# A hybrid decoder layer: gates of the recurrence in two groups of two chunks, 1/rms of the queries in the softmax's scale, that of the values in their copy, and the tail's last sum kept apart

## The chip, the cores and the metric

The kernel runs on one core of one Trainium2 chip. The metric is the device time of one execution in microseconds; of the kernel before there are three runs, and their median is compared. Besides the runs there is one profiled execution, whose trace gives every instruction of every engine with its start and its duration.

## The reference

The reference is one layer of a decoder trunk on x of 512 tokens by 1024 features, in float32:

```
x = x + 0.5 * rms_norm(swiglu(rms_norm(x, ..), ffn1_w_gu, ffn1_w_down), ..)
y = hybrid_mixer(rms_norm(x, mix_pre_g), w_in, ...)
x = x + rms_norm(y, mix_post_g)
x = x + 0.5 * rms_norm(swiglu(rms_norm(x, ..), ffn2_w_gu, ffn2_w_down), ..)
```

The mixer multiplies its normed input h by w_in and takes five parts out of the product: x_lru and gate_lru (512 columns each), q (8 heads of 64), k and v (2 heads of 64 each).

- The recurrence: a causal convolution of width 4 over x_lru gives xc; two block-diagonal products (8 blocks of 64 by 64) with a sigmoid give r and i; a = exp(8 r log_sigmoid(lambda)); u = sqrt(1 - a^2) * i * xc; then the scan h[t] = a[t] h[t-1] + u[t], times gelu(gate_lru).
- The attention: a sliding window of 128 over blocks of 128 queries, with a sink per head: m = max(max(scores), sink), p = exp(scores - m) / (sum + exp(sink - m)), and p times v.

Both results are normed, put side by side and multiplied by w_o.

rms_norm(x)[token] is x[token] * 1/rms(x[token]) * gain. The factor 1/rms is one number for each token, so q, k, v and x_lru of a token can all be computed from the input without it, and be multiplied by it afterwards. A score is q . k, so the factor of a query can as well stand in the scale of its row of scores; the factor of a value belongs to that value's row.

## The kernel before

Every product of float32 matrices is made of three matmuls of rounded halves: weights and activations are split into a high and a low part (ACT casts the high part, DVE or POOL subtracts it for the low part), and high*high, high*low and low*high are summed in PSUM (`mm3`, lines 505 to 507). The order of the instructions on each engine is written out by hand, in the order of the program; weights come through a list of units (`W.take`, `W.fill`), which loads, casts and splits a few units ahead. The loads go through SP's queue.

The feed-forward parts before and after the mixer are long rows of such products, in a form with seven products for eight. What is changed stands in the mixer and at the very end.

The mixer's first part keeps features on the partitions and tokens on the free axis, in tiles of 128x512:

- `boundary` ends with the four products of x_lru (tiles `an`), then PE computes k (`pk`), v (`pv`) and the four query products (`pq0` to `pq3`, two heads each), 24 matmuls of 512 columns each.
- `mx.R` holds 1/rms of every token, the same row on all partitions; `scaled(t, b)` is DVE's multiply of a product by it (line 1426). It is used for x_lru (line 1434), k, v and the four query tiles. `InvRms.invert` makes the factor first as a column per block of 128 tokens (`rs`, line 558), before it is turned into the row.
- `conv` (ACT line 1442, DVE line 1446) makes xc of two chunks of 128 channels at a time; `split_xc` (lines 1472 and 1473) makes its high part on ACT and its low part on POOL.
- `lru_gates(ci)` does one chunk: six matmuls (line 1454) whose weights lie in 64 of the 128 rows, the two halves of a chunk at the same time in the two halves of the array; two sigmoids on ACT (`r`, `other`); and because the halves of the two gates come out on the wrong partitions, two DMAs on SP's queue that gather `ig` (lines 1457 and 1459), POOL's product u = ig * xc (line 1461) and a DMA on POOL's queue that puts `other` into `r` (line 1462). It is called once for each chunk, after the query product of the same number.
- `in_parts` (lines 1426, 1486, 1492, 1493) scales a query or key product, copies its first block for the first block of the attention (tile `home`), and splits it. The low part of the last query tile is put off (`deferred`) until the attention has begun.
- After the first gates PE turns v (`vt`, line 1512), and DVE copies it into `home` (line 1514).
- The attention goes over 8 units (block b, group n of four heads): `scores` (PE products `cur` at line 1610 for the first block, `sc` at line 1621 for the others; DVE masks them, takes the maximum and makes `nm`, the negative of the maximum times the scale, line 1641), `exps` (ACT, line 1652, one for each head), `turn_p` (PE transposes, line 1664), `values` (lines 1683 and 1684). Between them PE does the products of the recurrence's gate (`gt`).

Small tiles of the tag "w" (`wt`) share 8 buffers in turn, so that a new one waits until the one before in its buffer is read; PSUM has 8 banks in the same manner.

The end of the kernel goes over four blocks of 128 tokens (tb). For each piece of the output DVE adds the last product to what was summed so far (`yp`, line 1983), ACT squares and sums it (line 1984), DVE or POOL multiplies by the gain (`last`, line 1988), and when all pieces are there: the sum of the sums (`tot`, lines 1986, 1990, 1992), the square root on ACT (1995), the reciprocal (1996) and the last multiply and add (1999) on DVE, and the store (2000). The last block has three pieces, of 512, 256 and 256 columns.

## Time and profile before

| what | value |
|---|---|
| median of three runs | 845.98 us (845.3 to 846.42) |
| span of the profiled execution, first to last instruction | 843.6 us |
| granted TensorE clock, mean | 0.998 |
| PE busy | 834.5 us, 99% of the span |
| DVE / ACT / POOL busy | 732.7 / 523.8 / 201.7 us |
| chain that ended last | 97% PE |

The profiled execution has no time of its own beside its span; what lies around the span is taken as the difference between the median of the runs and the span, 2.4 us.

Views of the trace used below: the page (spans, busy time, the chain that ended last), the chain in order of time (start, length, engine, tile, line), the timeline (start, length, engine, line, operation, output <- inputs, shapes, count; in brackets how long the engine was idle before and what ended that) and the list of one tile's instructions. A PE matmul row gives the time that one matmul is in the array, and matmuls overlap; their pace is read from the starts, or from the chain, where each stands with its share.

### The profile page before, as it was taken

The page shows a single profiled execution, that of the slowest core. Times are in us where ns is not written, and L with a number is a line of the kernel's source. Part 1 is how long each engine was busy: PE and PEld are TensorE (multiplying, and loading weights), DVE is VectorE, ACT ScalarE, POOL GpSimd, SP SyncE. Part 2 cuts the span into 40 slices and gives each one's busy share as a digit, 9 for nine tenths or more (in the row PEclk, how much of TensorE's full clock was granted, in tenths as well). Part 3 has the DMA queues.
Part 4 walks back from the last instruction along what each step waited for, and adds up shares of the span by engine and source line. Part 5 has one row for each costly group of instructions (what it writes and reads, how often), then busy time and mean ns, then how long its engine had stood idle before and what let it go on. Part 6 is the DMA issues. An engine that isn't in the chain of part 4 may idle for free.

```text
span 843.6 us, 12618 instructions
## 1 busy us (share of the span) xinstructions
PE 834.5 (99%) x4568; PEld 722.6 (86%) x4568; DVE 732.7 (87%) x1020; ACT 523.8 (62%) x874; POOL 201.7 (24%) x214
## 2 busy tenths in 40 slices
PE   9999999999999999999999999999999999999996
PEld 8988888988988998997788899888888888888885
DVE  4978999998979865889899589799998998998996
ACT  6646856666666655456788457436757767666552
POOL 2023000140320333334646055112004113032001
PEclk9999999999999999999999999999999999999999
DMA  7249419397595799222511131169539939769742
GB/s 251 77 131 348 151 59 322 80 254 254 129 248 185 169 261 343 77 79 91 158 50 51 50 110 42 50 137 273 186 108 231 322 91 249 249 154 262 295 137 101
DMA packets 123615, 143.75 MB, mean 170 GB/s; under 512 B 23896, under 2 KB 81568, under 8 KB 123040
## 3 DMA queue, kind: packets, MB, share of 16 engines
q1 hardware_dynamic: 109232, 111.86, 41.6%
q0 software_dynamic: 14176, 30.94, 17.0%
q8 instruction: 36, 0.59, 0.3%
q14 instruction: 27, 0.22, 0.1%
q10 hardware_dynamic: 144, 0.13, 0.0%
HBM read 100.45 MB, written 40.89 MB: 168 GB/s over the span
## 4 chain that ended last, share of the span: by engine, by line
PE 97%; ACT 1%; DVE 1%; DMA 1%; issue 0%; POOL 0%; DVEq 0%; POOLq 0%; ACTq 0%
PE ab L955 10%; PE aa L955 10%; PE da L955 5%; PE db L955 5%; PE yaa L1345 3%; PE bb L955 3%; PE ba L955 3%; PE yda L1345 2%; PE ya L507 2%; PE ya L505 2%; PE ya L506 2%; PE a_first L1205 1%; PE aa L885 1%; PE yab L1875 1%; PE yab L1874 1%; PE yab L1876 1%
## 5 line engine op out<-in xcount | busy, mean ns | idle before, releaser
L1115 POOL DMA_DIRECT2D yp_a<-stage x42 | 36.9, 1085 | 181.2 <-ACT stage L1112 160.9
L1115 POOL DMA_DIRECT2D yp_b<-stage x42 | 36.4, 1091 | 144.6 <-ACT stage L1112 121.1
L505 PE MATMUL ya<-hha,whi_ad 128*128 128x512 f32 x62 | 24.1, 389 | 0.0
L506 PE MATMUL ya<-hla,whi_ad 128*128 128x512 f32 x62 | 24.1, 389 | 0.0
L507 PE MATMUL ya<-hha,wlo_ad 128*128 128x512 f32 x62 | 24.1, 389 | 0.0
L688 POOL TENSOR_TENSOR acca_r<-acca_r,sq_r 128x512 f32<-128x512 f32 x6 | 8.2, 1359 | 51.4 <-ACT sq_r L536 51.4
L1988 POOL TENSOR_TENSOR last<-yp,grow 128x512 f32<-128x512 f32 x3 | 3.9, 1290 | 57.7 <-DVE yp L1983 57.7
L524 PE MATMUL an<-xh_mx,whi_xl 128*128 128x256 f32 x64 | 15.8, 287 | 0.0
L1984 ACT ACTIVATE ysq<-yp 128x512 f32<-128x512 f32 (+1 forms) x9 | 5.3, 585 | 16.5 <-DVE yp L1983 16.0
L525 PE MATMUL an<-xh_mx,wlo_xl 128*128 128x256 f32 x64 | 15.5, 283 | 0.0
L505 PE MATMUL gt<-xh_mx,whi_gt 128*128 128x512 f32 x32 | 14.2, 444 | 0.0
L1112 ACT COPY stage<-yab 128x512 f32<-128x512 f32 x12 | 6.5, 604 | 11.7 <-DMA yp_b<-stage 7.4
L507 PEld LDWEIGHTS ya<-hha,wlo_ad 128*128 128x128 f32 x62 | 11.6, 188 | 2.4
L506 PEld LDWEIGHTS ya<-hla,whi_ad 128*128 128x128 f32 x62 | 11.6, 188 | 2.4
L505 PEld LDWEIGHTS ya<-hha,whi_ad 128*128 128x128 f32 x62 | 11.6, 188 | 2.4
L536 ACT ACTIVATE sq_r<-yp_a 128x256 f32<-128x256 f32 (+1 forms) x10 | 5.0, 502 | 12.9 <-DVE yp_a L678 5.9
L505 PE MATMUL pq<-xh_mx,whi_q 128*128 128x512 f32 x32 | 12.8, 400 | 0.0
L505 PE MATMUL pub<-xh_f,whi_bu 128*128 128x512 f32 x32 | 12.6, 395 | 0.0
L507 PE MATMUL gt<-xh_mx,wlo_gt 128*128 128x512 f32 x32 | 12.6, 394 | 0.0
L505 PE MATMUL pgb<-xh_f,whi_bg 128*128 128x512 f32 x32 | 12.6, 393 | 0.0
L506 PE MATMUL gt<-xl_mx,whi_gt 128*128 128x512 f32 x32 | 12.5, 392 | 0.0
L580 ACT ACTIVATE xh_f<-xT,cols 128x256 fp32r<-128x256 f32 x16 | 8.1, 509 | 7.0 <-DVE xT L719 6.4
(2014 smaller groups left out, 3535.0 us busy)
## 6 DMA issues: line engine op xcount, KB each, us to landing
yp_a<-stage POOLq DMA_DIRECT2D x50, 256.0 KB, 8.9
yp_b<-stage POOLq DMA_DIRECT2D x50, 256.0 KB, 9.2
h_a<-za SPq DMA_DIRECT2D x16, 256.0 KB
hxa<-h_a SPq DMA_DIRECT2D x16, 256.0 KB
h_b<-zb SPq DMA_DIRECT2D x16, 256.0 KB
hxb<-h_b SPq DMA_DIRECT2D x16, 256.0 KB
xn<-in_x SPq DMA_DIRECT2D x8, 256.0 KB
xT_hbm<-xT POOLq DMA_DIRECT2D x2, 1024.0 KB, 9.7
```

Source lines behind the costliest of these rows:

```text
L505: pe.matmul(ps, hi[:, k, :], xh, start=start, stop=False)
L506: pe.matmul(ps, hi[:, k, :], xl, start=False, stop=False)
L507: pe.matmul(ps, lo[:, k, :], xh, start=False, stop=stop)
L524: pe.matmul(ps[:, sl], hi[:, k, :], xh, start=k == 0, stop=False)
L525: pe.matmul(ps[:, sl], lo[:, k, :], xh, start=False, stop=False)
L885: pe.matmul(o, w[:, k, js], x, start=first and i + j + k == 0, stop=k == 3 and i == 2, skip_group_check=True)
L955: pe.matmul(b[tb], x[:, blk], w[:, k, :], start=first and q + k + j == 0, stop=q + k == 2 and j == 2, skip_group_check=True)
L1115: pool.dma_start(o, st.rearrange("p (a b) -> p a b", a=2) if len(o.shape) == 3 else st, accum_op=ALU.add)
L1205: pe.matmul(banks[j][:, HALF[0]], ws[j][part][:, k, :], n1.xs[k][xpart][:, HALF[0]], start=k == 0 and part == xpart, stop=stop and k == KD ...
L1345: pe.matmul(o, a[:, k, ms], x[:, js], start=first and i + k + m % 2 == 0, stop=k == 1 and i == 2, skip_group_check=True)
L1874: pe.matmul(banks[i], hh[:, js], hi[:, k, :], start=first and k == 0, stop=False, skip_group_check=True)
L1875: pe.matmul(banks[i], hh[:, js], lo[:, k, :], start=False, stop=False, skip_group_check=True)
```

## The change

Four things are changed.

1. `lru_gates` takes a group of chunks. It issues the matmuls of both chunks, term by term, then all sigmoids and SP's DMAs of the group, then what is handed in as `between`, and last POOL's products and POOL's DMAs. It is called twice: chunks 0 and 1 after the first query product (with the splits of chunks 2 and 3 as `between`), chunks 2 and 3 after the third. The split of chunk 1 stands before v's product now.
2. The query products are no longer scaled: `in_parts` reads the PSUM bank directly. Three small tiles hold the column of 1/rms per block (`rows_scale`) and that times 1/8 and -1/8; `nm` and the exponentials take their scale from them.
3. v is copied out of PSUM by ACT (`act.copy`) without the scale, and the copy of the turned v into `home` multiplies by the column.
4. At the very end, the last piece's sum of squares has a tile of its own, the sum of the first two and the epsilon are made by DVE ahead as the bias of the square root, and the gain multiplies of the last two pieces stand behind the square root in the program.

```diff
--- before.py
+++ after.py
@@ -554,7 +554,7 @@
             n = self.name
             rms = small.tile([P, 2], F32, tag="rms", name=f"rms_s{n}")
             act.activation(rms, ms, AF.Sqrt, bias=self.eps, scale=scale)
-            rs = small.tile([P, 2], F32, tag="rs", name=f"rs_{n}")
+            rs = self.rs = small.tile([P, 2], F32, tag="rs", name=f"rs_{n}")
             dve.reciprocal(rs, rms)
             self.dg = wt(f"dg_{n}", T)[:, :2 * P].rearrange("p (a b) -> p a b", a=2)
             dve.tensor_tensor(self.dg, ident.unsqueeze(1).to_broadcast([P, 2, P]), rs.unsqueeze(2).to_broadcast([P, 2, P]), op=ALU.mult)
@@ -1445,25 +1445,32 @@
                 ci = c0 + j
                 dve.scalar_tensor_tensor(xcs[ci], xps[ci][:, 1 + w:1 + w + T], col("conv_w", w * KC + ci), xcs[ci], op0=ALU.mult, op1=ALU.add)
 
-    def lru_gates(ci):
-
-        banks = bank(f"rg{ci}"), bank(f"ig{ci}")
-        (hi, lo), (xh, xl) = gw["both"], xc_parts[ci]
-        for i, (w, x) in enumerate(((hi, xh), (hi, xl), (lo, xh))):
-            for ps, half in zip(banks, SIDE):
-                pe.matmul(ps, w[half, ci, :], x[half, :], start=i == 0, stop=i == 2)
-        r, other, ig = t2k(f"r{ci}"), wt(f"other{ci}"), wt(f"ig{ci}")
-        act.activation(r, banks[0], AF.Sigmoid, bias=col("b_rg", ci))
-        sync.dma_start(ig[SIDE[0], :], r[SIDE[1], :])
-        act.activation(other, banks[1], AF.Sigmoid, bias=col("b_ig", ci))
-        sync.dma_start(ig[SIDE[1], :], other[SIDE[0], :])
-        u = xcs[ci]
-        pool.tensor_mul(u, ig, u)
-        pool.dma_start(r[SIDE[1], :], other[SIDE[1], :])
-        t = t2k(f"th{ci}")
-        rs_.append(r)
-        us_.append(u)
-        th.append(t)
+    def lru_gates(cs, between=lambda: None):
+
+        banks = {ci: (bank(f"rg{ci}"), bank(f"ig{ci}")) for ci in cs}
+        hi, lo = gw["both"]
+        for i in range(3):
+            for ci in cs:
+                xh, xl = xc_parts[ci]
+                w, x = ((hi, xh), (hi, xl), (lo, xh))[i]
+                for ps, half in zip(banks[ci], SIDE):
+                    pe.matmul(ps, w[half, ci, :], x[half, :], start=i == 0, stop=i == 2)
+        gates = {}
+        for ci in cs:
+            r, other, ig = gates[ci] = t2k(f"r{ci}"), wt(f"other{ci}"), wt(f"ig{ci}")
+            act.activation(r, banks[ci][0], AF.Sigmoid, bias=col("b_rg", ci))
+            sync.dma_start(ig[SIDE[0], :], r[SIDE[1], :])
+            act.activation(other, banks[ci][1], AF.Sigmoid, bias=col("b_ig", ci))
+            sync.dma_start(ig[SIDE[1], :], other[SIDE[0], :])
+        between()
+        for ci in cs:
+            r, other, ig = gates[ci]
+            u = xcs[ci]
+            pool.tensor_mul(u, ig, u)
+            pool.dma_start(r[SIDE[1], :], other[SIDE[1], :])
+            rs_.append(r)
+            us_.append(u)
+            th.append(t2k(f"th{ci}"))
 
     xc_parts = {}
 
@@ -1480,9 +1487,18 @@
     xps = [conv_in(ci, b) for ci, b in enumerate(xl_banks)]
     k0, q0 = home[0][:, :P], home[0][:, T:2 * T]
 
+    rows_scale = const.tile([P, NB], F32, name="rows_scale")
+    score_scale = const.tile([P, NB], F32, name="score_scale")
+    minus_scale = const.tile([P, NB], F32, name="minus_scale")
+    for h in range(2):
+        blocks = slice(2 * h, 2 * h + 2)
+        dve.tensor_copy(rows_scale[:, blocks], mx.rms[h].rs)
+    dve.tensor_scalar(score_scale, rows_scale, HD ** -0.5, None, op0=ALU.mult)
+    dve.tensor_scalar(minus_scale, rows_scale, -HD ** -0.5, None, op0=ALU.mult)
+
     def in_parts(b, first, name, low=dve):
 
-        x = scaled(wt(name), b)
+        x = scaled(wt(name), b) if name == "kT" else b
         dve.tensor_copy(first, x[:, :P])
         if name == "qT3":
             spare.extend(fours("attn", F32R))
@@ -1496,22 +1512,25 @@
     conv(0, xps)
     split_xc(0)
     kT = in_parts(pk, k0, "kT", pool)
+    split_xc(1)
     pv = in_product("pv")
-    vT = scaled(wt("vT"), pv)
+    vT = wt("vT")
+    act.copy(vT, pv)
     conv(2, xps)
     qT = []
     for j in range(4):
         b = in_product(f"pq{j}")
-        if j < KC - 1:
-            split_xc(j + 1)
-        lru_gates(j)
+        if j == 0:
+            lru_gates((0, 1), lambda: (split_xc(2), split_xc(3)))
+        if j == 2:
+            lru_gates((2, 3))
         qT.append(in_parts(b, q0[:, j * P:(j + 1) * P], f"qT{j}", deferred if j == 3 else dve))
         if j == 0:
             vt = bank("vt")
             for b in range(NB):
                 pe.transpose(vt[:, b * P:(b + 1) * P], vT[:, b * P:(b + 1) * P], ident)
             v = home[0][:, 3 * T:]
-            dve.tensor_copy(v, vt)
+            dve.tensor_tensor(v4(v), v4(vt), rows_scale.unsqueeze(2).to_broadcast([P, NB, P]), op=ALU.mult)
     preload(AF.Exp)
 
 
@@ -1592,7 +1611,6 @@
         dve.tensor_tensor_scan(hl[ci], rs_[ci], us_[ci], initial=0.0, op0=ALU.mult, op1=ALU.add)
 
 
-    scale = HD ** -0.5
     yns = []
     ssq = const.tile([P, NB], F32, name="ssq")
     unit = {}
@@ -1638,7 +1656,7 @@
                 dve.tensor_reduce(mx_[:, 2 * i:2 * i + 2], cur, op=ALU.max, axis=AX.X)
                 heads += [both[:, j, 1, :] for j in range(2)]
         nm = small.tile([P, 4], F32, tag="nm", name=f"nm{b}{n}")
-        dve.scalar_tensor_tensor(nm, mx_, -scale, nsink[:, 4 * n:4 * n + 4], op0=ALU.mult, op1=ALU.min)
+        dve.scalar_tensor_tensor(nm, mx_, minus_scale[:, b:b + 1], nsink[:, 4 * n:4 * n + 4], op0=ALU.mult, op1=ALU.min)
         es = small.tile([P, 4], F32, tag="es", name=f"es{b}{n}")
         dve.tensor_add(es, nm, sinks[:, 4 * n:4 * n + 4])
         unit[b, n] = heads, nm, es
@@ -1649,7 +1667,7 @@
         sc = wt(f"sc{b}{n}")
         for j in range(4):
             hs = slice(j * P, (j + 1) * P)
-            act.activation(sc[:, hs], heads[j], AF.Exp, bias=nm[:, j:j + 1], scale=scale, accum_out=dsum[:, j:j + 1])
+            act.activation(sc[:, hs], heads[j], AF.Exp, bias=nm[:, j:j + 1], scale=score_scale[:, b:b + 1], accum_out=dsum[:, j:j + 1])
         act.activation(es, es, AF.Exp)
         if n == 0:
             unit[b] = small.tile([P, 8], F32, tag="den", name=f"den{b}")
@@ -1981,18 +1999,24 @@
             out_products(tb, i, range(f0 + 2 * ((tb, i) in started), f1))
             y = parts[tb, dh][:, c0:c1]
             dve.scalar_tensor_tensor(y, place(tb, i), -1.0 if dh else 1.0, y, op0=ALU.mult, op1=ALU.subtract if dh else ALU.add)
-            act.activation(wt(f"ysq{tb}{i}")[:, :c1 - c0], y, AF.Square, accum_out=ss[:, i:i + 1])
-            if end and i == 2:
-                dve.tensor_add(tot, ss[:, 0:1], ss[:, 1:2])
+            if i == 2:
+                ss_last = small.tile([P, 1], F32, tag="tot", name="ss_last")
+                act.activation(wt(f"ysq{tb}{i}")[:, :c1 - c0], y, AF.Square, accum_out=ss_last)
+                dve.tensor_scalar(tot, ss[:, 0:1], 4.0 / D, 4 * EPS, op0=ALU.mult, op1=ALU.add)
+                dve.scalar_tensor_tensor(tot, ss[:, 1:2], 4.0 / D, tot, op0=ALU.mult, op1=ALU.add)
+            else:
+                act.activation(wt(f"ysq{tb}{i}")[:, :c1 - c0], y, AF.Square, accum_out=ss[:, i:i + 1])
             last.append(wt(f"last{tb}{i}")[:, :c1 - c0])
-            (dve if end or i else pool).tensor_mul(last[i], y, grow[dh][:, c0:c1])
+            if not end or i == 0:
+                (dve if end or i else pool).tensor_mul(last[i], y, grow[dh][:, c0:c1])
+        rs = small.tile([P, 1], F32, tag="rs1", name=f"rs_b{tb}")
         if end:
-            dve.tensor_add(tot, tot, ss[:, 2:3])
+            act.activation(rs, ss_last, AF.Sqrt, bias=tot, scale=4.0 / D)
+            for i, (dh, c0, c1) in list(enumerate(pieces[tb]))[1:]:
+                dve.tensor_mul(last[i], parts[tb, dh][:, c0:c1], grow[dh][:, c0:c1])
         else:
             dve.tensor_add(tot, ss[:, 0:1], ss[:, 1:2])
-
-        rs = small.tile([P, 1], F32, tag="rs1", name=f"rs_b{tb}")
-        act.activation(rs, tot, AF.Sqrt, bias=eps4, scale=4.0 / D)
+            act.activation(rs, tot, AF.Sqrt, bias=eps4, scale=4.0 / D)
         dve.reciprocal(rs, rs)
         for i, (dh, c0, c1) in enumerate(pieces[tb]):
             y = parts[tb, dh][:, c0:c1]
```

## The prediction

> **What bounds the kernel now.** I read the page first, then the chain in order of time around the gates, then the timelines of ACT, POOL and DVE there, and last the chain of the tail. From the page:
>
> ```profile
> span 843.6 us, 12618 instructions
> ...
> PE 834.5 (99%) x4568; PEld 722.6 (86%) x4568; DVE 732.7 (87%) x1020; ACT 523.8 (62%) x874; POOL 201.7 (24%) x214
> ...
> PE 97%; ACT 1%; DVE 1%; DMA 1%; issue 0%; POOL 0%; DVEq 0%; POOLq 0%; ACTq 0%
> ```
>
> PE is the chain. Work taken off another engine gains nothing by itself; an edit counts where it changes PE's own row of instructions, makes PE wait or wait less, or stands behind PE's last matmul. What lies around the span is 845.98 - 843.6 = 2.4 us; I take it as unchanged, so every term below goes from the span to the median as it is.
>
> **Part 1: the gates' groups on PE.** The chain in order of time at the gates of chunk 1:
>
> ```profile
> 395.49 0.42 PE rg L1454
> 395.92 0.23 PE ig L1454
> 396.38 0.43 PE pq L505
> 396.81 0.23 PE pq L506
> ```
>
> A matmul of 512 columns takes 0.23 us of the chain (two gate matmuls, one in each half of the array, share it), but the first after a change between 128-row and 64-row weights takes 0.42 or 0.43. Going into the gates and out again costs 0.42 + 0.43 - 2 x 0.23 = 0.39 us. Before, PE goes in and out after pq0, pq1 and pq2; after pq3 the gates run straight into `cur`, which is 64-row too, so there is one way in and one way out of both together. After, it goes in and out behind pq0 and pq2, and pq3 goes straight into `cur`, again once in and out. One pair goes: **-0.39 us**. The 24 gate matmuls stay. Bounds: 0 (if a group of two breaks the sharing or the pair moves elsewhere) and -0.8 (if two pairs went, which the order of the instructions excludes).
>
> **Part 2: v copied by ACT.** PE turns v behind the first gates, now twelve matmuls instead of six, and waits for ACT's copy instead of DVE's multiply.
>
> ```profile
> 385.15 0.62 ACT L1492 CAST kTh<-kT 128x512 fp32r<-128x512 f32 x1 [0.58 <-DVE kT L1426]
> 385.67 2.00 ACT L209 CAST whi_q<-raw_q 128x1024 fp32r<-128x1024 f32 x2
> 387.57 1.04 ACT L209 CAST whi_gt<-raw_gt__4051 128x1024 fp32r<-128x1024 f32 x1
> 388.52 1.52 ACT L1442 ACTIVATE xc<-xp,cols 128x512 f32<-128x512 f32 x2
> ```
> ```profile
> 389.33 0.66 PE L1512 MATMUL vt<-ident,vT 128*128 128x128 f32 x4
> ```
>
> On DVE four tiny operations (the columns' copies and scales) now stand ahead of the convolution; a 128x1 operation takes 0.16 (row 838.24 below), and back to back they take less, so 0.45 in all (bounds 0.3 and 0.64). kTh slips by that to 385.60. From start to start ACT takes 0.52 for a cast of 512 columns and (387.57 - 385.67)/2 = 0.95 for one of 1024: the cast of chunk 1 (new here) starts at 386.12, two of whi_q at 386.64, whi_gt at 388.54, vT at 389.49, and vT is there at 389.49 + 0.62 = 390.1. PE would turn v at 389.33 + 3 x 0.23 = 390.0. **+0.1 us**, bounds 0 and 0.5. Chunk 1's low part on POOL (two operations of 1.3 ahead of it, done about 388.9) is wanted at 389.2: just covered.
>
> **Part 3: what the second group brings late.** This is the new wait that I take most seriously. `r3` and `other3` moved ahead of qT2's cast on ACT, and in the new order `other3` takes the buffer that `other1` had, which is free only when POOL's DMA of chunk 1 has read it. That DMA stands behind POOL's xcl2, xcl3, u0, its DMA, and u1. Behind `other3` on ACT stands qT2's high part; DVE waits for that with qT2's low part, then makes a wlo_gt of 1.2, and only then copies the first block of pq3, which PE's last matmuls of `cur` read. POOL's rows before, and the operations of DVE beside two of them, and the landing of the DMAs of `r` and `ig`:
>
> ```profile
> 396.66 1.31 POOL L1461 TENSOR_TENSOR xc<-ig,xc 128x512 f32<-128x512 f32 x1 [3.76 <-DMA ig<-other]
> 397.90 0.56 POOL L1462 DMA_DIRECT2D r<-other  x1
> 399.37 2.16 POOL L1473 TENSOR_TENSOR xcl<-xc,xch 128x512 fp32r<-128x512 f32 x1 [0.92 <-ACT xch L1472]
> 402.90 1.75 POOL L1461 TENSOR_TENSOR xc<-ig,xc 128x512 f32<-128x512 f32 x1 [1.36 <-DMA ig<-other]
> ...
> 407.07 2.36 POOL L1461 TENSOR_TENSOR xc<-ig,xc 128x512 f32<-128x512 f32 x1 [0.63 <-DMA ig<-other]
> ```
> ```profile
> 399.17 1.21 DVE L214 TENSOR_TENSOR wlo_gt<-raw_gt__4051,whi_gt 128x1024 fp32r<-128x1024 f32 x1
> ...
> 402.28 1.22 DVE L214 TENSOR_TENSOR wlo_gt<-raw_gt__4099,whi_gt 128x1024 fp32r<-128x1024 f32 x1
> ```
> ```profile
> DMA to landing us min/median/max: 2.3/2.9/3.1
> ```
>
> A POOL operation takes 1.3 alone and about 2.2 when a wlo_gt of DVE started just ahead of it. ACT after vT: two conv starts, a cast of 1024, the table load (1.28), four sigmoids at 0.59 from start to start, so chunk 2's high part starts at 396.1 and is there at 396.7. POOL: xcl2 to 398.1, xcl3 to 399.3; wlo_gt, due at 399.0, then holds u0 up from 399.3 to 400.5, u0 to 401.75, its DMA 0.55 to 402.3; the next wlo_gt (from 402.05) holds u1 up to 403.25, u1 to 404.5. POOL's DMA of chunk 1 starts there and lands 2.3 later, at 406.9. `other3` runs to 407.6 (0.68), qT2's high part to 408.1, its low part (from 408.2, 0.6 to the next) and wlo_gt (1.2, and 0.25 behind POOL's u2) to 410.3, the copy of 0.2 to 410.5. PE wants it for the last quarter of `cur`: pq3's last matmul starts at 408.7, `cur` runs about 1 us behind it, so its last quarter is due at 409.85. **+0.6 us**. Bounds: 0, where u0 and u1 take 1.3 each and the copy waits for pq3 alone; and 3.2, where both xcl take 2.16, both u 2.36 and the DMA 3.1 (landing at 409.5 and all behind it 2.6 later). I take the middle way because the two wlo_gt fall beside u0 and u1 by their own times.
>
> The skill weighs in here. The Trainium skill, "SBUF — State Buffer", section "Who interferes with whom", says that a DVE instruction with two SBUF inputs and a GpSimd instruction that reads SBUF exclude each other for the whole instruction, the first to start winning, while one with at most one SBUF input does not contend. By that rule the queries' low parts, which now read one operand from PSUM, leave POOL alone, and the wait stays 0.6; if they held POOL up as a wlo_gt does, two of them at 0.68 would make it about 2.0 and the sum +0.95. No row before shows such a pair overlapping.
>
> **Part 4: the first unit of the attention.** ACT's sigmoids of chunk 3 used to stand ahead of the exponential's table load; the first transposes waited for the exponentials:
>
> ```profile
> 413.85 0.74 PE L1664 MATMUL pt<-ident,sc 128*128 128x128 f32 x4
> ```
> ```profile
> 437.66 0.60 PE L1664 MATMUL pt<-ident,sc 128*128 128x128 f32 x4
> ```
>
> Unhindered the four take 0.60, here 0.74. The two sigmoids (1.2 us) are gone from this place, and the table load starts behind the cast of pq3: **-0.14 us** (bounds -0.14 and 0, the latter if part 3 delays that cast by more than a microsecond).
>
> **Part 5: five scale multiplies leave DVE, ACT gets a copy.** 5 x 0.68 = 3.4 us less on DVE, 0.6 more on ACT. Nothing on the path: PE runs on through all of them. The factor as a tile instead of a constant in `nm` and in the exponentials, and in v's second copy: the same shapes, **0** (bounds -0.1 and +0.3 for 32 exponentials at 0.01).
>
> **Part 6: the tail.** PE's last matmul, and then DVE and ACT:
>
> ```profile
> 836.39 0.28 PE L1852 MATMUL ybl<-whi_br,hlb 128*128 128x256 f32 x1
> ```
> ```profile
> 836.56 0.42 DVE L1988 TENSOR_TENSOR last<-yp,grow 128x256 f32<-128x256 f32 x1
> 836.91 0.42 DVE L1983 SCALAR_TENSOR_TENSOR yp<-ybl,yp 128x256 f32<-128x256 f32 x1
> 837.24 0.15 DVE L1986 TENSOR_TENSOR tot_b<-ss_b 128x1 f32<-128x1 f32 x1
> 837.36 0.43 DVE L1988 TENSOR_TENSOR last<-yp,grow 128x256 f32<-128x256 f32 x1
> 838.24 0.16 DVE L1990 TENSOR_TENSOR tot_b<-tot_b,ss_b 128x1 f32<-128x1 f32 x1 [0.45 <-ACT ysq L1984]
> 838.76 0.16 DVE L1996 RECIPROCAL rs_b<-rs_b 128x1 f32<-128x1 f32 x1 [0.36 <-ACT rs_b L1995]
> ```
> ```profile
> 837.70 0.42 ACT L1984 ACTIVATE ysq<-yp 128x256 f32<-128x256 f32 x1 [0.56 <-DVE tot_b L1986]
> 838.02 0.19 ACT L1984 ACTIVATION_READ_ACCUMULATOR ysq<-yp 128x1 f32 x1
> 838.43 0.29 ACT L1995 ACTIVATE rs_b<-tot_b,eps 128x1 f32<-128x1 f32 x1 [0.23 <-DVE tot_b L1990]
> ```
>
> All of this is on the path. (a) The last add waits behind a gain multiply; without it, it starts when PE is done, 836.7 instead of 836.91. (b) The square starts at 837.70 because it waits for a sum of the same tile; with a tile of its own it follows the add by 0.5, at 837.2. (c) The square root need not wait for DVE's last sum: 837.2 + 0.51 = 837.75 instead of 838.43. (d) The reciprocal follows by 0.33, at 838.1 instead of 838.76. What moves in between on DVE are two sums (0.16 each) and two gain multiplies (0.34 each from start to start), 837.1 to 838.1: they just fit, and may push the reciprocal by 0.05. **-0.62 us**, bounds -0.7 and -0.4.
>
> **The sum.** -0.39 + 0.1 + 0.6 - 0.14 + 0 - 0.62 = -0.45 us: a span of 843.6 - 0.45 = 843.15 and, with 2.4 around it, 845.5 us. All good ends give -0.39 - 0.14 - 0.7 = -1.2 (-1.3 with part 5's), all bad ends +3.6.
>
> **Rivals.**
> - *No wait at `cur`*: POOL gets through undisturbed, part 3 is 0: -1.05, 844.9 us. For it: u0 took 1.31 once. Against it: wlo_gt of 1.2 comes by at those times.
> - *The wait at `cur` takes the gain and more*: the same chain with POOL's long rows. Each microsecond that POOL's DMA of chunk 1 lands later than 406.3 costs PE one. The kernel is slower by over 0.2% (1.7 us) from a wait of 2.75 on, a landing at 409.0; at the full 3.2 it gives +2.15, 848.1 us. For it: 2.16 and 2.36 stand in the trace. Against it: all four operations would have to be long, and DVE has 3.4 us less to do.
> - *A stall of the late attention goes too*. ACT's two table loads make PE wait at the seventh unit:
>
> ```profile
> 442.41 1.38 PE L1664 MATMUL pt<-ident,sc 128*128 128x128 f32 x4 [0.28 <-ACT sc L1652]
> ```
> ```profile
> 434.38 0.37 ACT L1652 ACTIVATE sc<-sc,nm 128x128 f32<-128x128 f32 x1 [1.59 <-PE po L1683]
> ```
>
> The four transposes take 1.38 instead of 0.60 and start 0.45 late, 1.2 in all. If ACT came to them early by what it saves, this would go: -1.05 - 1.2 = -2.25, 843.7 us. Against it: the row of 434.38 shows ACT idle for 1.59 until PE is there, and what follows is ACT's own row; it moves with PE.
>
> **How the numbers follow.** My forecast (a short wait at `cur`) has 0.50, no wait there 0.22, the long wait 0.14, the late stall gone 0.14. The likeliest gives 845.5 (its own range 844.6 to 846.4). Leaving out the ends of the last two, the range is 843.8 to 847.4. 0.2% is 1.7 us, about what a measurement of this kernel can tell from no change: within it lie the first two and a part of the others, 0.74; faster 0.15, slower 0.11.
>
> **What would show it.** Right: one pair of 0.42 and 0.43 fewer in the chain between pq0 and `cur`; the last 1999 starting 0.6 us closer to PE's last matmul; `cur` longer than its 1 us with DVE's copy of pq3 as what PE waits for, and ACT's `other3` idle until POOL's DMA. Wrong: a wait of PE at the second group of gates or at `vt` of more than 0.5, exponentials longer than 0.35 to 0.38, or a stall of PE in the attention that differs from 1.2.

## The result and the profile after

The changed kernel takes 851.68 us (median of 4 executions, 851.31 to 854.97) against 845.68 for the kernel before: slower by a ratio of 1.0077, 95% interval 1.0061 to 1.0093. The forecast was 845.5, with 847.4 as the upper end of its range. The page of the changed kernel, the rows that answer to those shown of before:

```profile
span 853.3 us, 12607 instructions
...
PE 838.7 (98%) x4568; PEld 722.7 (85%) x4568; DVE 730.3 (86%) x1019; ACT 525.5 (62%) x875; POOL 200.9 (24%) x214
...
PE 62%; issue 14%; DMA 12%; DVE 5%; POOL 3%; ACT 3%; SPq 1%; DVEq 0%; POOLq 0%; ACTq 0%
```

PE was 97% of the chain before and is 62% now; DMA is 12% of it, most of that POOL's `yp_b<-stage` from 595 us on, where no line was changed. (In the second profile, e2 below, the chain is 75% PE and 6% DMA.) The profiled execution is the slowest of the four (854.97; the other three have spans of 849.6 to 850.3): PE waits 2 us at 318 us and then runs at half its pitch for about 3 us. The two windows below are the wait and what follows it; behind the length stand the busy times of PE, PEld, DVE, ACT and POOL, then PEclk (the granted clock), the DMA share and GB/s:

```profile
317.00:320.20 3.20, 1.50 (x7) 0.92 (x5) 1.45 (x3) 2.23 (x5) 0.00 (x0) 1.00 1.10 356
320.20:325.00 4.80, 4.63 (x13) 3.53 (x14) 3.52 (x6) 2.54 (x5) 0.00 (x0) 0.68 1.14 271
```

A second profile of the changed kernel (run e2 below, span 849.9) has a shorter wait there and no fall of the clock, so I compare that one with a second profile of the kernel before (run e1, span 843.8). In both kernels PE executes the same 4568 matmuls, so I cut the trace at the same matmuls: the first of `pv` opens the mixer, the first of `wo` closes its attention. In us, by the starts of these matmuls, counted from the start of the span (worked out from the trace):

| stretch | before (e1) | changed (e2) | difference |
|---|---|---|---|
| start to `pv` (no instruction changed) | 377.3 | 379.8 | +2.6 |
| `pv` to `wo` (gates, queries, attention) | 80.7 | 82.8 | +2.1 |
| `wo` to PE's last matmul (no instruction changed) | 378.6 | 380.8 | +2.2 |
| last matmul to the end of the span | 7.2 | 6.5 | -0.7 |

(The last row is from the two pages and the tails shown in the prediction and below, 843.6 - 836.39 and 853.3 - 846.77.) So 4.8 us come from stretches in which nothing was changed, 2.1 from the mixer, where I had expected +0.17 in all, and the tail gave back 0.7.

In the unchanged stretches the DMAs are slower. From the trace's record of every packet: the 8,192 packets of 512 bytes that the hardware queue moves between 100 and 300 us (pieces of weights, which are loaded as 128 columns of 4 bytes) take 32.3 ns on average in e1 and 37.5 in e2, and the 10,752 packets of 2 KB of POOL's queue (sums of products, added into memory) take 178.6 and 187.8. The 512-byte packets of the first 100 us are slower too (27.2 and 30.1), hundreds of microseconds before the first changed instruction.

In the mixer, the groups of the exponentials, before and after (minimum, median and maximum in ns of one):

```profile
L1652 ACT ACTIVATE sc<-sc,nm x24: 356/369/406, 419.7 to 447.0; 128x128 f32<-128x128 f32 x24
L1652 ACT ACTIVATE sc<-cur,nm x8: 350/370/381, 412.7 to 416.5; 128x128 f32<-128x128 f32 x8
```
```profile
L1670 ACT ACTIVATE sc<-sc,nm,score_scale x24: 447/458/487, 425.0 to 453.7; 128x128 f32<-128x128 f32 x24
L1670 ACT ACTIVATE sc<-cur,nm,score_scale x8: 446/458/469, 417.6 to 421.7; 128x128 f32<-128x128 f32 x8
```

Each got 0.09 us longer by taking its scale from a tile. The late stall at the seventh unit, 1.38 for the four transposes before, is now

```profile
448.62 1.65 PE L1682 MATMUL pt<-ident,sc 128*128 128x128 f32 x4 [0.55 <-ACT sc L1670]
```

And the wait at `cur` is there. PE's rows, before and after:

```profile
409.33 1.05 PE L1610 MATMUL cur<-home 64*128 64x128 f32 x16
410.31 0.50 PE L505 MATMUL gt<-xh_mx,whi_gt 128*128 128x512 f32 x1
```
```profile
413.84 0.94 PE L1628 MATMUL cur<-home 64*128 64x128 f32 x12
415.05 0.49 PE L1628 MATMUL cur<-home 64*128 64x128 f32 x4 [0.27 <-DVE home L1502]
415.47 0.50 PE L505 MATMUL gt<-xh_mx,whi_gt 128*128 128x512 f32 x1
```

The chain in order of time at that place (start, duration, what):

```profile
408.65 2.23 DMA r<-other
...
410.99 0.69 ACT other L1463
411.68 0.49 ACT qT2h L1508
...
412.19 0.69 DVE qT2l L1509
412.88 1.92 DVE wlo_gt L214
414.80 0.21 DVE home L1502
...
415.05 0.49 PE cur L1628 x4
```

It is link by link the chain of part 3 of the prediction: POOL's DMA of chunk 1, `other3`, the cast of the third queries, their low part, a `wlo_gt`, the copy, PE. From the first matmul of `cur` to the next product it is 1.63 us here and 1.48 in e2, against 0.98 before. One link is longer than forecast, `wlo_gt`, and these rows show beside what; the earlier pair is POOL's product u of chunk 1 with the `wlo_gt` before it:

```profile
407.21 2.60 DVE L214 TENSOR_TENSOR wlo_gt<-raw_gt__4110,whi_gt 128x1024 fp32r<-128x1024 f32 x1
412.19 0.69 DVE L1509 TENSOR_TENSOR qT2l<-pq,qT2h 128x512 fp32r<-128x512 f32 x1 [2.17 <-ACT qT2h L1508]
412.80 2.00 DVE L214 TENSOR_TENSOR wlo_gt<-raw_gt__4110,whi_gt 128x1024 fp32r<-128x1024 f32 x1
```
```profile
407.42 1.30 POOL L1469 TENSOR_TENSOR xc<-ig,xc 128x512 f32<-128x512 f32 x1
412.42 1.29 POOL L1469 TENSOR_TENSOR xc<-ig,xc 128x512 f32<-128x512 f32 x1 [3.23 <-DMA ig<-other]
```

POOL's products take 1.3, as alone; both `wlo_gt`, 1.21 alone, end 1.09 us behind the product beside them. The low part `qT2l`, which reads one operand from PSUM, runs beside the second product and neither is longer than alone.

The tail, PE's last matmul and the engines behind it:

```profile
846.77 0.28 PE L1870 MATMUL ybl<-whi_br,hlb 128*128 128x256 f32 x1
```
```profile
847.09 0.42 DVE L2001 SCALAR_TENSOR_TENSOR yp<-ybl,yp 128x256 f32<-128x256 f32 x1 [0.18 <-PE ybl L1870]
...
848.42 0.15 DVE L2020 RECIPROCAL rs_b<-rs_b 128x1 f32<-128x1 f32 x1
848.61 1.54 DVE L2023 SCALAR_TENSOR_TENSOR yp<-last,rs_b,x_rows 128x512 f32<-128x512 f32 x3
```
```profile
847.55 0.42 ACT L2004 ACTIVATE ysq<-yp 128x256 f32<-128x256 f32 x1
...
848.09 0.29 ACT L2014 ACTIVATE rs_b<-ss_last,tot_b 128x1 f32<-128x1 f32 x1
```

The last step starts 848.61 - 846.77 = 1.84 us behind PE's last matmul; before it was 838.96 - 836.39 = 2.57.

### The profile page after: what moved, and what is told of

It reads as the page before. It is cut to its first block, busy times and chain, and to the rows that moved or that the text cites. A ratio compares the mean times of both kernels' runs of the same rounds, so it can differ in the third digit from the quotient of the medians.

```text
span 853.3 us, 12607 instructions
## 1 busy us (share of the span) xinstructions
PE 838.7 (98%) x4568; PEld 722.7 (85%) x4568; DVE 730.3 (86%) x1019; ACT 525.5 (62%) x875; POOL 200.9 (24%) x214
## 4 chain that ended last, share of the span: by engine, by line
PE 62%; issue 14%; DMA 12%; DVE 5%; POOL 3%; ACT 3%; SPq 1%; DVEq 0%; POOLq 0%; ACTq 0%
PE aa L955 10%; DMA yp_b<-stage 8%; PE da L955 5%; PE yaa L1345 3%; PE ba L955 3%; PE yda L1345 2%; PE ab L955 2%; DMA raw_ad__3210<-in_ffn_w_down 2%; PE ya L505 2%; PE ya L506 2%; PE ya L507 2%; POOL yp_b L1115 1%; PE wo L1823 1%; DMA raw_second<-in_ffn_w_gu 1%; PE yea L1345 1%
## 5 line engine op out<-in xcount | busy, mean ns | idle before, releaser
L831 ACT CAST hhs<-s4b 128x512 fp32r<-128x512 f32 x4 | 2.5, 621 | 16.3 <-DVE s4b L867 16.3
```

## The experiments

First four kernels together: are the slow packets a matter of the chip and the execution, or of the program; what do the exponentials cost; what does the tail give? Each ratio is to the kernel before, measured beside it on the same chip, with its 95% interval.

**e1, the kernel before once more.** No edit.

> The kernel before, unchanged, once more. In the trace of the changed kernel the DMA packets of 512 bytes take 38.5 ns on average between 100 and 300 us, in that of before 31.7, though the instructions there are the same; and the changed kernel stalls PE by 0.65 us at the first matmul of `ab` in each of four blocks from 603 us on, before does not. Theory A: the pace of the packets belongs to the chip or to the execution and not to the kernel; then this run can show 38 ns too, with the four stalls and 2 to 4 us more than 845.7. Theory B: it belongs to the program as changed (where its data or its code lies); then this run shows 31.7 ns, no stall of that kind, and 845.3 to 846.4.

845.46 us, ratio 1.0001 (0.9992 to 1.0010); packets of 512 bytes 32.3 ns, no new stall of PE (of the 4568 matmuls all but 11, which lie in the first 8 us, start within 0.5 us of their place in the first profile).

**e2, the changed kernel once more.** No edit.

> The changed kernel, unchanged, once more. Its profiled execution lost 3.7 us between 317 and 325 us (PE waits 2.0 and then runs at a pitch of 0.427 for eight matmuls); its other executions had a span of 849.6 to 850.3, so I expect that stall to be gone here: span 849.6, time 851.3. Theory A (pace of the packets by execution or chip): 512-byte packets at the same mean as in the run of the kernel before on this chip. Theory B (by the program): 38 ns again, and the four stalls of 0.65 us again.

851.79 us, ratio 1.0080 (1.0066 to 1.0094); packets 37.5 ns. On one chip, side by side, the two programs differ as they did: the pace belongs to the program. Theory B holds, and the question becomes what in the program sets it.

**e3, the exponentials with the constant scale.** The kernel leaves out the queries' 1/rms; `nm` has its constant back as well.

```
-  nm ... mx_, minus_scale[:, b:b + 1], ...
+  nm ... mx_, -HD ** -0.5, ...
-  act.activation(..., AF.Exp, bias=nm[:, j:j + 1], scale=score_scale[:, b:b + 1], ...)
+  act.activation(..., AF.Exp, bias=nm[:, j:j + 1], scale=HD ** -0.5, ...)
```

> The changed kernel, but the exponentials and `nm` take the constant 1/8 (HD to the power -0.5) as scale instead of a column of a tile; the factor 1/rms of the queries is left out, all else is as changed. Theory 1 (an exponential with its scale in a tile takes 0.44 us from start to start instead of 0.345, and that is what lengthens the attention): 32 exponentials at 0.345 again, the stall of PE at the transposes of the seventh and eighth unit shorter by 1.0 to 1.5 us, no wait of 0.6 at the scores of the third block, time 1.0 to 1.6 us below the changed kernel's in this call. Rival (the exponentials run beside PE, and the attention is late because the second group of gates is late): exponentials shorter, time within 0.4 us of the changed kernel's.

849.32 us, 2.47 below e2 (ratio 1.0051, 1.0037 to 1.0065). The exponentials:

```profile
L1670 ACT ACTIVATE sc<-sc,nm x24: 359/372/407, 421.0 to 448.2; 128x128 f32<-128x128 f32 x24
```

are at 372 ns again, and `pv` to `wo` takes 80.1 instead of 82.8. Theory 1 holds and was too low: 2.5 instead of 1.0 to 1.6. By the starts of PE's matmuls in the two traces it is 0.3 at the first transposes, 0.8 at the scores of the third block and 0.2 to 0.45 at each of five later places. A part of it can be `nm`, which takes 0.16 us again instead of 0.22 in each of eight units; the run does not part the two. The packets stay slow (38.4 ns).

**e4, the new tail alone.** The kernel before with the last hunk of the diff.

> The kernel before with the new tail alone. Theory 1 (the tail gains what was worked out): from PE's last matmul to the end of the span 0.6 us less (7.2 to 6.6), time 845.0 to 845.2 with the packets of 512 bytes at the same pace as in the kernel before in this call. Rival (the pace of the packets follows each newly built program): the tail gains 0.6, but the packets take 34 ns or more and the time is at or above that of the kernel before.

844.85 us, 0.62 below before (ratio 0.9994, 0.9985 to 1.0003, so the time alone does not tell it from no change), packets 32.3 ns. The trace does: from PE's last matmul to the issue of the last store it takes 839.30 - 836.27 = 3.03 us, before 840.14 - 836.39 = 3.75. A newly built program alone does not slow the packets.

What remained for the packets: the changed kernel allocates three tiles of 16 bytes a partition in the first pool of SBUF, which takes them in steps of 32. In the compiled program every tile of 2 KB and every weight tile behind that pool therefore starts 96 bytes later: the first at byte 18,528 of a partition instead of 18,432, that is at 96 modulo 512 instead of 0. The next four kernels test this.

**e5, the kernel before with 96 unused bytes.**

```
+  const.tile([P, 24], F32, name="pad")
```

> The kernel before with one unused tile of 96 bytes a partition allocated where the changed kernel allocates its three columns of scales (32 bytes each in the allocator's steps). No instruction is added or moved; every weight tile and every tile of 2 KB starts 96 bytes later, at 96 modulo 512 instead of 0. Theory 1 (the place of the tiles slows the DMA's packets): packets of 512 bytes take 38 ns instead of 31.8, the stall at 318 us and the four of 0.65 us at `ab` are there, time 4 to 5 us above the kernel before. Rival (the pace follows something else in the changed kernel, its new instructions or their order): 31.8 ns, no such stalls, 845.5.

850.17 us, 4.68 above before (ratio 1.0058, 1.0044 to 1.0072), without one instruction more. Packets of 512 bytes 37.9 ns, of POOL's queue 186.1 (32.3 and 178.6 in e1). The page's part on the queues, share of 16 engines, for e1 and e5:

```profile
q1 hardware_dynamic: 109232, 111.86, 41.6%
q0 software_dynamic: 14176, 30.94, 17.1%
```
```profile
q1 hardware_dynamic: 109232, 111.86, 42.3%
q0 software_dynamic: 14176, 30.94, 17.7%
```

Same packets, same bytes, more time. Where it reaches PE is shown by the waits. Between 300 and 322 us and in the first of four like blocks (645 to 660 us here, 640 to 655 in e1), first e1 and then e5 (engine, line, what it waited for: us in total, times, longest):

```profile
ACT whi_ad L209 <- DMA raw_ad__3210<-in_ffn_w_down: 5.0, 1, 5.0
...
ACT stage L1112 <- DMA yp_b<-stage: 3.8, 1, 3.8
```
```profile
ACT whi_ad L209 <- DMA raw_ad__3210<-in_ffn_w_down: 6.8, 1, 6.8
PE ya L505 <- ACT hha L892: 1.1, 1, 1.1
...
ACT stage L1112 <- DMA yp_b<-stage: 5.4, 1, 5.4
PE ab L955 <- ACT bb L960: 0.4, 1, 0.4
```

ACT waits for its weights 1.8 us longer and PE then waits for ACT; in the blocks ACT waits for a buffer that POOL's accumulating DMA still reads, and PE waits for the copy that stands behind it on ACT. In e1 neither row of PE appears. The engines' own instructions are not slower at the new place: DVE is busy for 732.3 us (732.4 in e1), ACT for 521.1 (524.3) and POOL for 200.9 (202.4). Theory 1 is shown: the place alone costs 4.7 us. (The traced execution, the quickest of five with 849.27, has 3.8 of it: 2.0 ahead of `pv` and 1.9 behind `wo`.)

**e6, 128 unused bytes.** The same line with 32 columns.

> The kernel before with an unused tile of 128 bytes: the tiles start at 128 modulo 512, which is 0 modulo 64. Rival A (what counts is a start at a multiple of 64 bytes): packets of 512 bytes at 31.8 ns, time as before, 845.5. Rival B (what counts is a start at a multiple of 256 or 512 bytes): 38 ns or more, and 4 us or more above before. By the Trainium skill, DMA: Bandwidth & Descriptors, How a descriptor splits into AXI transactions, an estimate: 512 bytes from 128 on take 20 beats instead of 16, 39.8 ns; at 96 they take 19, 37.8 ns (the traces of the changed kernel have 37.2 to 38.5).

846.95 us, 1.46 above before (ratio 1.0019, 1.0010 to 1.0029). Packets of 512 bytes 36.2 ns, but those of POOL's queue 178.7, as before:

```profile
q1 hardware_dynamic: 109232, 111.86, 42.4%
q0 software_dynamic: 14176, 30.94, 17.1%
```

Neither rival: there are two effects. The 512-byte pieces are slow at 128 as they are at 96; the accumulating DMA is slow at 96 and not at 128. By the time, 1.5 us against 4.7, the second weighs more here; no run has the second without the first.

**e7, the changed kernel with its three columns elsewhere.**

```
-  rows_scale = const.tile([P, NB], F32, name="rows_scale")
+  rows_scale = small.tile([P, NB], F32, tag="rows_scale", name="rows_scale", bufs=1)
   (and so for score_scale and minus_scale)
```

> The changed kernel with its three columns of scales taken from the last pool of SBUF instead of the first, so that all weight tiles and tiles of 2 KB lie where they lie in the kernel before; the instructions and their order are those of the changed kernel. Theory 1: packets of 512 bytes at 31.8 ns, no stall at 318 us and none at `ab`; what is left above the kernel before is the longer exponentials less the tail and the gates: +2.0 in the mixer, -0.6 in the tail, 846.5 to 847.3. Rival (the place is not the cause): 851.8 as the changed kernel.

846.61 us (ratio 1.0013, 1.0004 to 1.0022), 5.2 below e2; packets 32.3 and 178.3 ns, no stall of PE at 318 us nor at the blocks. Theory 1 is shown from this side too. The first transposes take 1.18 us here instead of e2's 0.67: DVE's masking copy on `cur` takes 1.55, beside POOL's product of chunk 3, and 1.02 in e2.

**e8, the same, with the queries multiplied by 1/rms on DVE as before and the constant scale.**

```
-  x = scaled(wt(name), b) if name == "kT" else b
+  x = scaled(wt(name), b)
```

> The changed kernel with the tiles where they lie before, and with the queries multiplied by 1/rms on DVE as before, so that the exponentials have the constant scale again; the gates in two groups, the copy of v and the tail stay as changed. Theory 1 (two causes, place and exponentials, make all of the loss): exponentials at 0.345 from start to start, packets of 512 bytes at 31.8 ns; gates -0.39, tail -0.6, a wait at `cur` of 0.5 to 1.2 (DVE has four multiplies of 0.68 more), 844.7 to 845.5. Rival (the second group of gates alone makes the attention late): 846.5 or more.

850.45 us (ratio 1.0060, 1.0047 to 1.0073): my expectation failed. The gates' two groups and the queries' own buffers do not go together:

```profile
400.17 0.69 DVE L1426 TENSOR_TENSOR qT<-pq,R_mx 128x512 f32<-128x512 f32 x1 [3.67 <-POOL xc L1469]
```
```profile
412.54 0.80 PE L1624 MATMUL cur<-home 64*128 64x128 f32 x4 [3.26 <-DVE home L1498]
```
```profile
412.40:418.80 6.40, 6.26 (x17) 4.88 (x18) 5.31 (x11) 3.22 (x12) 2.42 (x5) 0.50 0.92 286
```

The first multiply of the queries wants a 2 KB buffer that POOL's u0 still holds; DVE stands for 3.67 us, everything behind it is late, `cur` waits 3.26, and PE is granted half its clock (0.50 in the last row) for the next 6 us. So the unscaled queries were what made room for the groups.

**e9, e7 with the constant scale.** The edit of e3 on e7; it too leaves out the queries' 1/rms.

> The changed kernel with the tiles where they lie before and with the constant 1/8 as the exponentials' scale (the factor 1/rms of the queries is left out): what stays of the change are the gates in two groups, the copy of v, the queries read straight from PSUM, and the tail. Theory (the loss is the place and the exponentials, and nothing else): gates -0.39, vt +0.1, wait at `cur` +0.4, first transposes -0.14, tail -0.6: 844.7 to 845.0. Rival (the second group costs the attention more than the wait at `cur`): 845.5 or more.

844.49 us (ratio 0.9987, 0.9978 to 0.9996), 0.2 better than expected. With the place and the exponentials out, the rest of the change gains 0.9, of which the tail alone gave 0.6 in e4.

**e10, e8 with the product written back to its PSUM bank.**

```
-  x = scaled(wt(name), b)
+  x = scaled(wt(name) if name == "kT" else b, b)
```

> As the run in which DVE multiplies the queries by 1/rms and the exponentials keep the constant scale, but the product is written back to its PSUM bank, so that no 2 KB buffer is needed. Theory (in that run the multiply of the first queries waited 3.7 us for a buffer that POOL's u0 and its DMA still held, and this made `cur` wait 3.5 us and PE run at a pitch of 0.427 behind it): that wait of DVE is gone, `cur` waits 0.5 to 1.2 (a multiply of 0.69 stands ahead of the copy it waits for), no half pitch, 845.0 to 845.8. Rival (DVE's four multiplies are what is too much): `cur` waits 2 us or more, 848 or more.

845.45 us (ratio 0.9999, 0.9991 to 1.0008). DVE's wait and the half clock are gone, `cur` takes 1.61. The theory holds. What keeps it from gaining, beside `cur`, is that the first transposes take 1.13 from the first of them to PE's next matmul, 0.50 before: POOL's product of chunk 3 (from 410.35 on) now runs beside DVE's masking copy on `cur` (L1643, from 410.07 on), which takes 2.14 here and 0.70 in e14, where that product starts at 413.71.

A third share lies at the end: from PE's last matmul to the end of the span it takes 6.9 us here and 6.5 in e4, with the same tail. DVE idles 0.45 us before the third block's last multiplies, a wait that e14 does not have, and is late from there on. The trace puts the wait down to DVE's own reciprocal; its cause stays open.

**e11, e10 with ACT's cast of the third queries ahead of the second group's sigmoids.**

```
-  if j == 2: lru_gates((2, 3))
   qT.append(in_parts(...))
+  if j == 2: lru_gates((2, 3))
```

> The same, with ACT's cast of the third queries ahead of the sigmoids of the second group instead of behind them (no other instruction moves). Theory (the wait at `cur` comes over this cast, which stands behind the sigmoid that waits for POOL's DMA, and over DVE, which waits for the cast): no wait at `cur`, its copy done when the product ends, 844.3 to 844.9, below the kernel before. Rival (DVE's own rows are what `cur` waits for): within 0.3 us of the run without this move.

845.67 us (ratio 1.0001, 0.9992 to 1.0010), `cur` 1.61 as in e10: the rival holds here. DVE's rows for the last queries show what replaced the chain:

```profile
408.95 0.70 DVE L1426 TENSOR_TENSOR pq<-pq,R_mx 128x512 f32<-128x512 f32 x1 [0.40 <-PE pq L507]
409.69 0.29 DVE L1498 COPY home<-pq 128x128 f32<-128x128 f32 x1
```

DVE waits for PE, not for ACT. The multiply and the copy take 1.0 us behind the last product, and the twelve matmuls of `cur` that do not need them cover 0.66.

**e12, 32 unused bytes.** The line of e5 with 8 columns.

> The kernel before with an unused tile of 32 bytes a partition: the tiles start at 32 modulo 512. At 96 the packets of 512 bytes took 37.9 ns, at 128 they took 36.2, at 0 they take 31.8. Theory A (each 512 bytes that start off a multiple of 256 need a third transaction, and this is most of the price whatever the offset): 36 to 38 ns, 1.5 to 4.7 us above before. Theory B (the price grows with the bytes that are fetched in vain): little, 33 to 34 ns, less than 1.5 us above before; the Trainium skill, DMA: Bandwidth & Descriptors, How a descriptor splits into AXI transactions, gives 17 beats instead of 16 here, an estimate of 33.8 ns.

850.62 us, 5.2 above before (ratio 1.0061, 1.0048 to 1.0074); 512-byte packets 35.7 ns, POOL's 185.0. Theory B falls, by the packets (33 to 34 expected) and by the time. Theory A's bounds are missed too, by 0.3 ns and 0.5 us: the time is as bad at 32 as at 96. By packet of 512 bytes 0, 32, 96 and 128 bytes gave 32.3, 35.7, 37.9 and 36.2 ns; by packet of POOL's queue 178.6, 185.0, 186.1 and 178.7. The Trainium skill, "DMA: Bandwidth & Descriptors", section "How a descriptor splits into AXI transactions", says that a descriptor off a multiple of 256 bytes fetches from the boundary below it, so that the bytes ahead of its start cost beats too. The section speaks of what is fetched; the side that was moved here is the one that a load writes. By its beats, scaled from the 32.3 ns of e1, an estimate is 38.4 at 96, 34.3 at 32 and 40.4 at 128: that agrees in sign, and nearly in size at 96, but not at 32 and 128; the measurement decides. It has nothing on the second effect.

Open was still which chain sets the wait at `cur`, and whether the second group is worth having.

**e13, e7 with the edit of e11.** Queries unscaled, scale in a tile, cast ahead of the sigmoids.

> The changed kernel with the tiles where they lie before, and with ACT's cast of the third queries ahead of the second group's sigmoids; nothing else is moved. In the run without this move DVE waited 2.13 us for that cast, then made its low part and a wlo_gt of 1.98, and `cur` waited 0.37 for the copy behind it. Theory A (the chain over the cast sets the wait): DVE is done with wlo_gt before the last queries' product ends, the copy follows the product by 0.3, which `cur`'s first twelve matmuls of 0.66 cover: no wait at `cur`, 846.0 to 846.3. Theory B (POOL's slow neighbours on DVE set it): wlo_gt stays at 2 us beside POOL, the wait stays, 846.6.

In its trace the wait is gone. The last two queries' rows on DVE:

```profile
406.12 1.22 DVE L214 TENSOR_TENSOR wlo_gt<-raw_gt__4110,whi_gt 128x1024 fp32r<-128x1024 f32 x1
408.83 0.29 DVE L1502 COPY home<-pq 128x128 f32<-128x128 f32 x1 [1.50 <-PE pq L507]
```

`cur` takes 1.09 instead of e7's 1.51, and `pv` to `wo` 82.5 instead of 83.4: that fits theory A for the changed kernel, but it does not exclude theory B: with the move `wlo_gt` no longer meets a product of POOL and takes 1.22 instead of 1.98, and these 0.76 are more than the 0.42 that `cur` gained; the run does not part the late cast from POOL's hold on `wlo_gt`. The time doesn't show the gain: the profiled execution took 846.28, but the median of eleven is 846.98 (845.98 to 848.42), ratio 1.0022 (1.0013 to 1.0030), so the expected 846.0 to 846.3 was missed. Why its executions spread more than e7's (846.07 to 847.09) I can't tell from one trace; that stays open.

**e14, e10 with only chunks 0 and 1 in a group.**

```
-  if j == 2:
-      lru_gates((2, 3))
+  if j >= 2:
+      lru_gates((j,))
```

> As the run with the queries multiplied in their PSUM bank, but only chunks 0 and 1 have their gates in one group; those of chunk 2 and of chunk 3 stand behind the third and the fourth queries again, as in the kernel before. PE's row of weight changes is as in the changed kernel (one pair fewer than before), the gates of chunk 3 stand between the last queries and `cur` again. Theory (the second group costs what it uncovers: the copy of the last queries, and POOL's products that now run beside the first scores): no wait at `cur`, no 0.8 us at the first transposes, 844.3 to 844.8, below the kernel before and the kernel with the new tail alone. Rival (the first group costs as much as it saves): 844.85 or more, as with the tail alone.

843.81 us, ratio 0.9984 (0.9975 to 0.9993): faster than the kernel before, 0.5 better than the lower end expected. `cur` takes 1.04, the first transposes 0.39 (0.50 before), `pv` to `wo` 80.1. Against e1 the trace has 0.6 us of the gain in the mixer and 0.8 behind PE's last matmul. PE's rows there:

```profile
408.73 0.39 PE L1457 MATMUL rg<-xch,gates 64*128 64x512 f32 x1
408.73 0.39 PE L1457 MATMUL ig<-xch,gates 64*128 64x512 f32 x1
408.96 1.11 PE L1624 MATMUL cur<-home 64*128 64x128 f32 x16
```

The gates of chunk 3 stand between the last queries and `cur` again and cover multiply and copy; the pair of weight changes that the grouping saves is saved by the first group alone.

## Why the prediction was wrong

Point by point, by the prediction's own steps; measured from the traces of e1 and e2 unless another is named.

| step | forecast | measured |
|---|---|---|
| 1 and 2, first matmul of the queries to first of `cur` | -0.39 + 0.1 | 26.40 to 25.95: -0.45 |
| 3, wait at `cur` | +0.6 | 0.98 to 1.48 (1.63 in the first profile): +0.5 |
| 4, first transposes | -0.14 | 0.50 to 0.67: +0.17 (1.18 in e7); with the constant scale (e3) 0.35: -0.15 |
| 5, `nm` and exponentials with the scale in a tile | 0, at most +0.3 | e2 against e3: +2.5 |
| 6, tail | -0.62 | -0.7; by the median of e4 -0.62 |
| place of the tiles | not there | e5: +4.7; e2 against e7: +5.2 |

Steps 1, 2 and 6 were right in mechanism and size. The wait at `cur`, the most delicate, came over the forecast chain, and in e13 it goes with the move of the cast; but that its size came out is partly luck. Taken back by the 5.03 us by which `pv` starts later, POOL's DMA of chunk 1 landed at 405.85, 1.05 ahead of the forecast, mostly because the second `wlo_gt` did not hold POOL's u1 up: u1 took 1.30 and `wlo_gt` 2.60. The `wlo_gt` in the chain took 1.92, not 1.2 plus 0.25, and PE wanted the copy 0.4 earlier than forecast. The errors cancel. Part 3 also left open whether low parts that read from PSUM hold POOL up: they don't (`qT2l` at 412.19).

What failed is two things. First, part 5: the scale as a tile was put at "the same shapes, **0** (bounds -0.1 and +0.3 for 32 exponentials at 0.01)". I priced an operand's kind by its shape; that longer exponentials would show the forecast wrong I had written, but without a price. From start to start an exponential and the read of its sum went from 0.345 to 0.44, so 32 x 0.095 = 3.0 us more on ACT, besides 0.06 for each `nm` on DVE, and 2.5 us came through to the time, because transposes and scores wait for single exponentials in the very stretch where part 4 and the third rival had seen PE waiting for ACT. This also ate part 4's gain. The Trainium skill, "ScalarE: Activation LUTs", section "What ACT_TABLE_LOAD costs", states about 93 ns for each operand of one value a partition; the trace agrees with 89 (458 less 369).

Second, and larger, a term that was not in the sum: three small tiles moved every tile behind them by 96 bytes, and with that 4.7 us of waits for slower DMAs came to PE, where no line of the diff lies. I had listed the three tiles as operations on DVE and not as places in memory. The forecast that "PE is the chain" hid it: DMAs that just keep ahead of PE need only 1.8 us more to be late (raw_ad, 5.0 to 6.8).

With the place at +4.7, the scale in a tile at +2.5, the tail at -0.6 and the rest of the mixer at -0.4 (e9 less e4: 844.49 - 844.85, not measured side by side) the sum is +6.2; measured +6.0, and +6.3 between e1 and e2. Other pairs give 5.2 for the place (e2 less e7) and 2.1 for the scale (e7 less e9), so each is known to half a microsecond. Of the rivals, none named either cause. The long wait at `cur` gave the right sign with a wrong mechanism for this kernel (it did come in e8), no rival looked at an unchanged stretch, and the late stall did not go but grew: from the first transpose to PE's next matmul it was 1.13 and is 1.41 at the seventh unit, 0.79 and 1.16 at the eighth.

## What to carry to other kernels

A new small tile is also a shift of everything allocated behind it: put it in the last pool, or compare the addresses of the tiles that DMAs read and write, before the time of an edit is argued from its instructions. Price an operand's kind (a constant or a column of a tile) apart from its shape, and look for the cost on the engine for which others wait. When a block is moved off the place between a product and its reader, count what it covered there: here the cheapest form keeps the last block where it was and groups only the first two.

## What the runs showed of the hardware

- Transfers depend on where the SBUF side starts: 512-byte packets took 32.3 ns at a multiple of 512, 35.7 to 37.9 at 32, 96 and 128 beyond it; the packets of the accumulating queue took 178.6 ns at 0 and 178.7 at 128, 185.0 to 187.8 at 32 and 96. That was 1.5 to 5.2 us of 845 here.
- One operand more that is a column of a tile costs an exponential of 128x128 0.09 us.
- PE at half its pitch (0.427 us for 512 columns instead of 0.227) followed a gap of 2.25 us between two matmuls' starts in the first profile and one of 3.5 us in e8 (granted clock 0.50 over 6.4 us); a gap of 1.98 us at the same place in e2 was not followed by it. In the first profile PE lost 4.0 us against e1 there, by a wait of 2.0.
- The `wlo_gt` of DVE, with both operands in SBUF, took 1.22 where POOL stood still (e10, e13) and 1.9 to 2.6 beside POOL's products (changed kernel, e7), ending 1.09 us behind the product; the product took its usual 1.3. In the prediction it was mostly POOL's rows that were taken to grow. A low part with one operand in PSUM took 0.69 beside a product of 1.29: no wait on either side.
